# Three changes of order in a hybrid decoder block: ticks of the recurrent heads, weight casts at two gate borders, and weight sums in the first feed-forward product

## The chip, the cores and the metric

The kernel runs on one core of a Trainium2 chip, in one launch. The metric is the device time of one execution in microseconds (us). The time before is 2270.74 us, the median of three runs (2270.26 to 2275.47).

## The reference

One decoder layer on x of 512 tokens by 2048 columns, all in float32. A conditioning vector c gives six rows of shift, scale and gate. A normalised and modulated x goes through one projection whose columns feed two head groups: eight heads of dilated causal attention and eight heads of a gated linear recurrence (HGRN2, state 128). The heads' outputs, the recurrent ones normalised and multiplied by a gate, go through an output projection and a gated residual. Then follows a feed-forward part with the square of ReLU.

```python
def reference(x, c, ...):
    ...
    h = rms_norm(x, norm1_w[l]) * (1.0 + scale1) + shift1
    aq, ak, av, gq, gf, gi, gg = jnp.split(h @ w_in[l], split_at, axis=-1)
    attn = rms_norm(dilated_attention(rope(norm(aq)), rope(norm(ak)), av), attn_out_norm_w[l])
    hg = rms_norm(hgrn2(gq, gf, gi, lb), hg_norm_w[l]) * silu(gg)
    x = x + gate1 * (concatenate([attn, hg]) @ w_out[l])
    h2 = rms_norm(x, norm2_w[l]) * (1.0 + scale2) + shift2
    x = x + gate2 * (square(relu(h2 @ w_ff1[l])) @ w_ff2[l])
```

(The listing is shortened; helper names stand for the reference's own steps.)

## The kernel before, in words

**Products in three parts.** Every large product is made of float32 operands split into a high part (a cast, on ScalarE) and a low part (source minus high part, a subtraction on VectorE). TensorE multiplies high by high, high by low and low by high. `load_w` (line 189) loads two rows of weight tiles at a time, casts them (line 39, `whi`) and makes their low parts (line 40, `wlo`); four pairs of high and low parts exist at a time.

**Projections and ticks.** `project` (line 372) runs over sixteen k; each k is 12 matmuls of 512 columns into four PSUM banks (lines 202 to 204). After each k it calls `tick`, which advances the first generator of the list `tasks` by one step, up to its next `yield`; when a generator ends, the same tick goes on to the next one. A finished projection's banks are copied out by ScalarE (lines 411, 571, 712), and the next projection's first matmuls need those banks. TensorE's instructions run in the order in which the program is written (`manual_schedule`, line 850); so the yields decide between which matmuls a head's blocks stand. The order on the other engines is made at build time by a scheduler that works through a simulated timeline by priorities (`high_priority` raises one); `issue_after(x)` forbids that what is traced inside it, on x's engine, is placed ahead of x.

**A recurrent head** (`hgrn_head`, line 587) builds decay products level by level on VectorE (`z`, lines 603 to 619), and takes twelve ticks: three levels; the blocks of `pA` from the first three levels (line 584); three more; `pB`; one more; `pC` and `pD` with copies on ScalarE; an empty one; `pE` with the copy `far_sb` (line 684); the output product `pho` (line 692). `hgrn` runs four heads. The queue of tasks is the first group of recurrent heads, four attention heads (`attention`, line 449, with three empty ticks in front by `lead`), the second recurrent group, four more attention heads, a norm, `hg_out(0)`, `attention_out` and `hg_out(1)`. `hg_out` and `attention_out` turn finished columns (`to_mix`, line 551, matmuls on `ptm`, then ScalarE's scaled copy `mix`); `split_mix` (line 393) makes high and low parts of a `mix`, the stationary operand of the output projection. The first group's ticks lie beside three projections, 48 ticks; the second group's beside the next but two.

**The two gate borders.** `hg_gate` (line 706) projects the gate columns, once per group. Its four banks are copied by ScalarE (line 712). The first is followed by the second `hg_gate`, the second by `project_out(0)`, the first quarter of the output projection (line 878). There the operand of k = 0 is the first mix.

**The feed-forward products.** After four blocks of the plain kind, both products use a form of seven products for four (Strassen-Winograd). A block has seven parts, in the order 1, 5, 6, 7, 3, 4, 2, each of 48 matmuls (lines 1196 to 1198). Parts 5, 6, 7 and 4 first need a sum of weight tiles (`sum_of`, line 1161, VectorE line 1164), four sums to a part (u = 0 to 3); `part` (line 1166) then makes the high part (ScalarE, line 1180, `vhi`) and the low part (VectorE, line 1181, `vlo`). Each u has one pair of buffers, so a part's high part waits until the matmuls of the part before have read that u. The first product has six such blocks (2 to 7), of which block 2 is called `first` and has its sums behind the eighth low part; the second product follows with blocks of its own. Results are turned and made into forms in between (`turn`, `make_forms`), partly on VectorE, also as steps of `tasks`.

Of the kernel before, what the change touches and what calls it, by code (L numbers as in the profile page):

```python
# [44 lines left out]
def hybrid_block(ctx, tc, x, c, positions, norm1_w, w_ada, b_ada, w_in, q_norm_w, k_norm_w,  # L45
# [140 lines left out]
        nc.sync.dma_start(dst.rearrange("o (r p) -> (o r) p", p=P), row[0:NK, 0:P])  # L186
        yield

    def load_w(view, k0, c0, n=512, eng=None, ahead=True, raws=None, behind=False):
        with tc.high_priority() if ahead else ExitStack():  # L190
            raw = wr.tile([P, 2, n], F32, name="wraw", tag="raw", bufs=4)
            with tc.issue_after(marks[-3].ins) if behind else ExitStack():
                nc.sync.dma_start(raw, view[:, k0:k0 + 2, c0:c0 + n])
            if raws is not None:
                raws[:] = [raw[:, 0], raw[:, 1]]
            return [_split(nc, wr, raw[:, j], n, eng if j else None) for j in range(2)]

    def tok_mm(banks, hi, lo, whi, wlo, first, last):

# [172 lines left out]
    def project(c0, mm, rate=1.85, after=None):  # L372

        banks = [bank("prj", tag="mm") for _ in range(4)]
        for k0 in range(0, NK, 2):
            for j, (whi, wlo) in enumerate(load_w(win_v, k0, c0, 512, None, behind=len(marks) > 2)):
                k = k0 + j
                mm(banks, hhi[k], hlo[k], whi, wlo, k == 0, k == NK - 1)
                tick()
                owed[0] += rate  # L380
                while owed[0] >= 1.0:
                    bg_step()
                    owed[0] -= 1.0
                if after:
                    after(k)
            marks.append(asked[0])
        return banks
# [58 lines left out]
        bgw.insert(0, qk_norm(ts, i, rs))  # L446
        return ts if i else (ts, rs)

    def attention(qr, ks, vs, lead=0):
        qs, rsq = qr  # L450

        place = {3: (0, 0), 2: (1, 0), 0: (1, 384), 1: (2, 0)}

        def heads_t(h):
            tT = []
            for i, src in enumerate((qs, ks)):
                pt = bank("ptq")
                for ti in range(NT):
                    pe.transpose(pt[:, ti * P:(ti + 1) * P], src[ti][:, h * DH:(h + 1) * DH], ident)
                t = work("qT")  # L460
                act.activation(t, pt, AF.Copy, scale=wcol[:, i:i + 1])
                tT.append(t)
            return tT

        def scores(h, qT, kT):
            lsum = sm.tile([P, NT], F32, name="lsum")
            m = sm.tile([P, NT], F32, name="m")
            ps_s = [bank("pscore") for _ in range(3)]
            s_sb = [work("s_sb") for _ in range(3)]
            for ti in (3, 2, 0, 1):  # L470
                n = (ti + 1) * P
                b, o = place[ti]
                pe.matmul(ps_s[b][:, o:o + n], lhsT=qT[:, ti * P:(ti + 1) * P], rhs=kT[:, 0:n], start=True, stop=True)
            for ti in (3, 2, 0, 1):
                n = (ti + 1) * P
                b, o = place[ti]
                s = s_sb[b][:, o:o + n]
                with tc.high_priority(offset=400):
                    dve.scalar_tensor_tensor(s, ps_s[b][:, o:o + n], rsq[:, ti, h:h + 1], lnc_sb[:, 512 - n:512],
                                             op0=ALU.mult, op1=ALU.add)  # L480
                    dve.tensor_reduce(m[:, ti:ti + 1], s, axis=AX.X, op=ALU.max)
                    dve.tensor_scalar(m[:, ti:ti + 1], m[:, ti:ti + 1], -1.0, None, op0=ALU.mult)
                    act.activation(s, s, AF.Exp, bias=m[:, ti:ti + 1], accum_out=lsum[:, ti:ti + 1])
            return s_sb, lsum

        def weights_t(s_sb):
            p_sb = []
            for b, tis in enumerate(((3,), (2, 0), (1,))):
                pT = bank("pT")
                p_sb.append(work("p_sb"))  # L490
                for ti in tis:
                    o = place[ti][1]
                    for sj in range(ti + 1):
                        c = slice(o + sj * P, o + (sj + 1) * P)
                        pe.transpose(pT[:, c], s_sb[b][:, c], ident)
                n = 256 if b == 2 else 512
                act.copy(p_sb[b][:, 0:n], pT[:, 0:n])
            return p_sb

        def values(h, p_sb, lsum):  # L500
            hs = slice(h * DH, (h + 1) * DH)
            po = bank("po")
            for ti in range(NT):
                b, o = place[ti]
                for sj in range(ti + 1):
                    pe.matmul(po[:, ti * P:(ti + 1) * P], lhsT=p_sb[b][:, o + sj * P:o + (sj + 1) * P],
                              rhs=vs[sj][:, hs], start=sj == 0, stop=sj == ti)
            dve.reciprocal(lsum, lsum)
            for ti in range(NT):
                dve.tensor_scalar(qs[ti][:, hs], po[:, ti * P:(ti + 1) * P], lsum[:, ti:ti + 1], None, op0=ALU.mult)  # L510

        for _ in range(lead):
            yield
        tT = heads_t(0)
        yield
        p_sb = None
        for h in range(4):
            if h:
                values(h - 1, p_sb, lsum)
            s_sb, lsum = scores(h, *tT)  # L520
            for _ in range(4):
                yield
            p_sb = weights_t(s_sb)
            yield
            if h < 3:
                tT = heads_t(h + 1)
                yield
        values(3, p_sb, lsum)
        yield
# [54 lines left out]
            pe.matmul(dst[r0:r0 + 32, (b // 4) * 32:(b // 4) * 32 + 32], lhsT=lhs[:, bs], rhs=rhs[:, bs],  # L584
                      start=True, stop=True)

    def hgrn_head(h, f, q, vs, ss):


        hs = slice(h * DH, (h + 1) * DH)  # L590
# [41 lines left out]
        z2 = level(2)  # L632
        yield
        z4 = level(4)
        yield
        pA = bank("pA").rearrange("p (l b t) -> p l b t", l=4, t=32)
        flat = lambda t: t.rearrange("p b t -> p (b t)")
        for i, (l, r) in enumerate(((kk, q), (z1, z1), (z2, z2), (z4, z4))):
# [44 lines left out]
            pe.matmul(pE[:, u * 256:(u + 1) * 256], lhsT=z256[:, u * P:(u + 1) * P], rhs=z256[:, 256:512], start=True, stop=True)  # L683
        act.copy(far_sb[:, 2:6].rearrange("p b t -> p (b t)"), pE)
        yield
        tile_of = {(i, i): AT[:, i] for i in range(4)}
        for i, at in enumerate(((0, 1), (2, 3), (0, 2), (0, 3), (1, 2), (1, 3))):
            tile_of[at] = far_sb[:, i]
# [8 lines left out]
            act.activation(q[:, t], f[:, t], AF.Square, accum_out=ss[:, h, ti:ti + 1])  # L697
        yield

    def hgrn(fs, qs, vs, rs):  # L700
        ss = sm.tile([P, 4, NT], F32, name="hss", bufs=2)
        for h in range(4):
            yield from hgrn_head(h, fs[h], qs[h], vs, ss)
        rstd_of(rs.rearrange("p t h -> p (t h)"), ss.rearrange("p t h -> p (t h)"), 16, 1.0 / DH)

    def hg_gate(ht):
        gb = project(6144 + ht * 512, tok_mm, after=split_early if ht else None)
        gs = []
        for ti in range(NT):
            g = slot("gg")  # L710
            with tc.high_priority():
                act.copy(g, gb[ti])  # L712
            gs.append(g)
        for g in gs:
            sg = wk.tile([P, 512], F32, name="sg", tag="ev", bufs=2)
            act.activation(sg, g, AF.Tanh, scale=0.5)
            dve.tensor_scalar(sg, sg, 0.5, 0.5, op0=ALU.mult, op1=ALU.add)
            dve.tensor_tensor(g, g, sg, op=ALU.mult)
        return gs
# [133 lines left out]
    while bgw:  # L853
        bg_step()
    bgw[:] = later
    tasks.append(hgrn(f0, hq0, hv0, hrs[0]))
    q0 = qk(0, "aq", 0)
    k0_ = qk(1024, "ak", 1)
    v0 = evac(project(2048, tok_mm), "av")
    tasks.append(attention(q0, k0_, v0, 3))  # L860
    hq1 = hgrn_q(1)
    hv1 = evac(project(5120 + 512, tok_mm), "gi")
    tasks.append(hgrn(f1, hq1, hv1, hrs[1]))
# [14 lines left out]
    def project_out(q, rate, after):  # L878
        banks = [bank("prj", tag="bg" if q % 2 and i < 2 else "mm") for i in range(4)]
        for i0 in range(0, NK, 2):  # L880
            for j, (whi, wlo) in enumerate(load_w(wout_v, korder[i0], q * 512)):
                i = i0 + j
                while q == 0 and len(mixp) <= i:
                    if not split_mix():
# [273 lines left out]

    split_done, cast_done, loads = [], [], []

    def sum_of(dst, a, b, first):

        with tc.issue_after(split_done[7].ins) if first else ExitStack():
            dve.tensor_tensor(dst, a, b, op=ALU.subtract)  # L1164

    def part(i, u, w, first):

        b11, b12, b21, b22 = (w[u, e, n] for e in range(2) for n in range(2))
        if i == 5:
            sum_of(b11, b12, b11, first)  # L1170
        if i == 6:
            sum_of(b11, b22, b11, first)
        if i == 7:
            sum_of(b12, b22, b12, first)
        if i == 4:
            sum_of(b11, b11, b21, first)
        src = {1: b11, 5: b11, 6: b11, 4: b11, 7: b12, 2: b21, 3: b22}[i]
        hi = pools[f"spl{u}"].tile([P, 2, 512], F32R, name="vhi")
        lo = pools[f"spl{u}"].tile([P, 2, 512], F32R, name="vlo")
        cast_done.append(act.copy(hi, src))  # L1180
        split_done.append(dve.tensor_tensor(lo, src, hi.bitcast(F32), op=ALU.subtract))  # L1181
        return hi, lo
# [136 lines left out]
    def part_of(item):  # L1319
# [6 lines left out]

        def call(u):
            with tc.high_priority() if first and j < 2 else ExitStack():
                return part(i, u, w, first)
        return call  # L1330

    def order_of(item):
# [107 lines left out]
```

## Time and profile before

| | before |
|---|---|
| median of three runs | 2270.74 us (2270.26 to 2275.47) |
| the profiled execution | 2268.98 us |
| its span | 2267.1 us |
| TensorE's mean granted clock | 0.997 |
| instructions | 33088 |

PE is TensorE, DVE VectorE, ACT ScalarE, POOL GpSimd, SP the engine that issues most loads. A row of the waits says which engine and line waited for whose instruction, then the total in us, the number of waits and the longest. A row of a timeline gives start, duration, engine, line, operation, written and read tiles, and in brackets the idle time ahead and what ended it; equal neighbours are merged (x4). A row of the windows gives the stretch, its length, the busy time of PE, PEld (weight loads), DVE, ACT and POOL, the granted clock of PE, the DMA share and GB/s. Matmuls overlap: one is listed with 0.39 us and the next starts 0.23 us after it.

### The profile page before, as it was taken

The numbers are of one execution on the slowest core, as the hardware profiler recorded it, in microseconds if no ns is written. First come the engines' busy times: TensorE is split into PE (matmuls) and PEld (weight loads), VectorE is DVE, ScalarE is ACT, GpSimd is POOL, SyncE is SP. The second block draws the span as 40 slices with busy tenths as digits, with TensorE's granted clock in tenths as the row PEclk, the third lists the DMA queues.
The fourth block names the chain that finished last, engine by engine and source line by source line (L and its number), as shares of the span: only waits on it lengthen the run. The fifth ranks groups of instructions, "written<-read, shape, count | busy, mean of one in ns | idle before, by whom it ended". The sixth has DMA issues, their size and how long they took to land.

```text
span 2267.1 us, 33088 instructions
## 1 busy us (share of the span) xinstructions
PE 2212.1 (98%) x11769; PEld 1824.7 (80%) x11769; DVE 1808.9 (80%) x2765; ACT 1097.5 (48%) x1950; POOL 439.1 (19%) x664
## 2 busy tenths in 40 slices
PE   4999999999999999999999999999999999999999
PEld 3788787888888888888888888888888888888887
DVE  6998878688876557778658988898897779967878
ACT  5555334443453464457545555564564333443332
POOL 1000022000220000003232323333232222222221
PEclk9999999999999999999999999999999999999999
DMA  9797564566555248737879789889889987998884
GB/s 327 255 333 254 185 197 145 173 199 209 183 167 182 66 152 281 272 115 270 319 283 363 279 309 385 298 290 366 328 292 371 362 315 260 349 346 311 306 294 166
DMA packets 262581, 598.30 MB, mean 264 GB/s; under 512 B 23220, under 2 KB 43968, under 8 KB 262416
## 3 DMA queue, kind: packets, MB, share of 16 engines
q1 hardware_dynamic: 186800, 332.54, 43.2%
q0 software_dynamic: 70720, 254.21, 30.4%
q10 hardware_dynamic: 4896, 9.44, 1.2%
q8 instruction: 93, 1.52, 0.3%
q14 instruction: 72, 0.59, 0.1%
HBM read 518.49 MB, written 77.61 MB: 263 GB/s over the span
## 4 chain that ended last, share of the span: by engine, by line
PE 67%; issue 12%; DMA 9%; DVE 8%; POOL 3%; ACT 1%; SPq 0%; POOLq 0%; DVEq 0%; ACTq 0%
PE f L1198 8%; PE f L1197 8%; PE f L1196 8%; PE prj L202 8%; PE prj L204 8%; PE prj L203 8%; DMA f_lod<-fs 2%; PE f L212 2%; PE f L210 2%; PE f L211 2%; PE prj L211 2%; PE prj L212 2%; PE prj L210 2%; DVE vlo L1181 2%; DMA Fl<-h_lod 2%
## 5 line engine op out<-in xcount | busy, mean ns | idle before, releaser
L1180 ACT CAST vhi<-raw 128x1024 fp32r<-128x1024 f32 x392 | 413.5, 1056 | 534.0 <-PE f L1198 421.9
L1181 DVE TENSOR_TENSOR vlo<-raw,vhi 128x1024 fp32r<-128x1024 f32 x392 | 478.5, 1226 | 150.1 <-ACT vhi L1180 149.3
L1197 PE MATMUL f<-vlo,Fh 128*128 128x512 f32 x1376 | 536.9, 390 | 2.4 <-DVE vlo L1181 2.3
L1198 PE MATMUL f<-vhi,Fl 128*128 128x512 f32 x1376 | 535.7, 389 | 0.9 <-DMA Fl<-f_lod 0.9
L1196 PE MATMUL f<-vhi,Fh 128*128 128x512 f32 x1376 | 536.1, 390 | 0.0
L39 ACT CAST whi<-wraw 128x512 fp32r<-128x512 f32 (+1 forms) x368 | 220.7, 602 | 464.8 <-PE prj L204 330.9
L40 DVE TENSOR_TENSOR wlo<-wraw,whi 128x512 fp32r<-128x512 f32 (+1 forms) x368 | 245.7, 671 | 181.8 <-ACT whi L39 170.5
L202 PE MATMUL prj<-whi,hi 128*128 128x512 f32 x896 | 360.7, 403 | 1.8 <-ACT gg L712 1.7
L204 PE MATMUL prj<-whi,lo 128*128 128x512 f32 x896 | 350.7, 391 | 0.0
L203 PE MATMUL prj<-wlo,hi 128*128 128x512 f32 x896 | 349.8, 390 | 0.0
L1197 PEld LDWEIGHTS f<-vlo,Fh 128*128 128x128 f32 x1376 | 258.3, 188 | 61.0 <-DVE vlo L1181 7.7
L1198 PEld LDWEIGHTS f<-vhi,Fl 128*128 128x128 f32 x1376 | 258.3, 188 | 54.8 <-DMA Fl<-f_lod 1.4
L1196 PEld LDWEIGHTS f<-vhi,Fh 128*128 128x128 f32 x1376 | 258.3, 188 | 53.4
L1164 DVE TENSOR_TENSOR raw<-raw,raw 128x1024 f32<-128x1024 f32 x224 | 269.6, 1225 | 3.3 <-DMA raw<-in_w_ff_dram 2.9
L132 DVE SCALAR_TENSOR_TENSOR acc<-araw,sc,acc 128x512 f32<-128x512 f32 (+1 forms) x392 | 250.4, 677 | 22.9 <-DMA araw<-in_w_ada_dram 22.2
L202 PEld LDWEIGHTS prj<-whi,hi 128*128 128x128 f32 x896 | 168.9, 189 | 36.6 <-ACT gg L712 2.9
L204 PEld LDWEIGHTS prj<-whi,lo 128*128 128x128 f32 x896 | 168.6, 188 | 36.9 <-DVE lo L244 0.3
L203 PEld LDWEIGHTS prj<-wlo,hi 128*128 128x128 f32 x896 | 169.1, 189 | 32.7
L1142 POOL DMA_DIRECT2D Fh<-f_hid x112 | 79.0, 705 | 423.9 <-PE f L1198 410.2
L212 PE MATMUL f<-hi,wlo 128*128 128x512 f32 x256 | 99.9, 390 | 1.0 <-DVE wlo L40 1.0
L210 PE MATMUL f<-hi,whi 128*128 128x512 f32 x256 | 100.3, 392 | 0.0
L211 PE MATMUL f<-lo,whi 128*128 128x512 f32 x256 | 99.6, 389 | 0.0
(311 smaller groups left out, 2910.5 us busy)
## 6 DMA issues: line engine op xcount, KB each, us to landing
raw<-in_w_ff_dram SPq DMA_DIRECT2D x224, 512.0 KB, 10.5
araw<-in_w_ada_dram SPq DMA_DIRECT2D x384, 256.0 KB, 4.6
Fh<-f_hid POOLq DMA_DIRECT2D x112, 512.0 KB, 6.7
Fl<-f_lod POOLq DMA_DIRECT2D x112, 512.0 KB, 7.9
wraw<-in_w_in_dram SPq DMA_DIRECT2D x104, 512.0 KB, 5.0
Fh<-h_hid POOLq DMA_DIRECT2D x60, 512.0 KB, 6.5
Fl<-h_lod POOLq DMA_DIRECT2D x60, 512.0 KB, 7.5
f_hid<-part POOLq DMA_DIRECT2D x48, 512.0 KB, 8.1
```

The costliest lines, as they stand in the source:

```text
L39: nc.scalar.copy(hi, src)
L40: _split.low = (eng or nc.vector).tensor_tensor(lo, src, hi.bitcast(F32), op=ALU.subtract)
L132: dve.scalar_tensor_tensor(acc, raw[:, k - k0], vec[:, k:k + 1], acc, op0=ALU.mult, op1=ALU.add)
L202: pe.matmul(banks[ti], lhsT=hi[:, ts], rhs=whi, start=first, stop=False)
L203: pe.matmul(banks[ti], lhsT=hi[:, ts], rhs=wlo, start=False, stop=False)
L204: pe.matmul(banks[ti], lhsT=lo[:, ts], rhs=whi, start=False, stop=last)
L1164: dve.tensor_tensor(dst, a, b, op=ALU.subtract)
L1180: cast_done.append(act.copy(hi, src))
L1181: split_done.append(dve.tensor_tensor(lo, src, hi.bitcast(F32), op=ALU.subtract))
L1196: pe.matmul(banks[t], lhsT=fh[u][a][:, ts], rhs=whi[:, a], start=first, stop=False)
L1197: pe.matmul(banks[t], lhsT=fh[u][a][:, ts], rhs=wlo[:, a], start=False, stop=False)
L1198: pe.matmul(banks[t], lhsT=fl[u][a][:, ts], rhs=whi[:, a], start=False, stop=end)
```

## The change

Four edits, none of which adds or removes an instruction of the computation.

- `hgrn` takes a `lead` for its first head: the first group's first head has three more empty ticks between its third level and the blocks of `pA`. The first attention group's three empty ticks at its start are taken out.
- The third head (h = 2) of each recurrent group has one more empty tick between `pE` with its copy and the output product.
- `load_w` can place its two casts (and no other instruction) behind the last bank copy of the gate projection made last (`evacuated`). It is used for the second pair of k in every `project` after the first gate, which is the second gate's, and in `project_out(0)`.
- In all blocks of the first feed-forward product but the first one, each weight sum is placed behind the low part made two before it.

```diff
-    def load_w(view, k0, c0, n=512, eng=None, ahead=True, raws=None, behind=False):
+    evacuated = []
+
+    def load_w(view, k0, c0, n=512, eng=None, ahead=True, raws=None, behind=False, cast_behind=False):
...
-            return [_split(nc, wr, raw[:, j], n, eng if j else None) for j in range(2)]
+            with tc.issue_after(evacuated[0].ins) if cast_behind and evacuated else ExitStack():
+                return [_split(nc, wr, raw[:, j], n, eng if j else None) for j in range(2)]
...
-            for j, (whi, wlo) in enumerate(load_w(win_v, k0, c0, 512, None, behind=len(marks) > 2)):
+            for j, (whi, wlo) in enumerate(load_w(win_v, k0, c0, 512, None, behind=len(marks) > 2, cast_behind=k0 == 2)):
...
-    def attention(qr, ks, vs, lead=0):
+    def attention(qr, ks, vs):
...
-        for _ in range(lead):
-            yield
         tT = heads_t(0)
...
-    def hgrn_head(h, f, q, vs, ss):
+    def hgrn_head(h, f, q, vs, ss, lead):
...
         z4 = level(4)
-        yield
+        for _ in range(1 + lead):
+            yield
...
         act.copy(far_sb[:, 2:6].rearrange("p b t -> p (b t)"), pE)
         yield
+        if h == 2:
+            yield
...
-            yield from hgrn_head(h, fs[h], qs[h], vs, ss)
+            yield from hgrn_head(h, fs[h], qs[h], vs, ss, 0 if h else lead)
...
-                act.copy(g, gb[ti])
+                evacuated[:] = [act.copy(g, gb[ti])]
...
-    tasks.append(hgrn(f0, hq0, hv0, hrs[0]))
+    tasks.append(hgrn(f0, hq0, hv0, hrs[0], 3))
...
-    tasks.append(attention(q0, k0_, v0, 3))
+    tasks.append(attention(q0, k0_, v0))
...
-            for j, (whi, wlo) in enumerate(load_w(wout_v, korder[i0], q * 512)):
+            for j, (whi, wlo) in enumerate(load_w(wout_v, korder[i0], q * 512, cast_behind=q == 0 and i0 == 2)):
...
-    def sum_of(dst, a, b, first):
+    def sum_of(dst, a, b, first, tie):
 
-        with tc.issue_after(split_done[7].ins) if first else ExitStack():
+        with tc.issue_after(split_done[7 if first else -2].ins) if first or tie else ExitStack():
             dve.tensor_tensor(dst, a, b, op=ALU.subtract)
...
-                return part(i, u, w, first)
+                return part(i, u, w, first, stage_ == 1)
```

(The four calls of `sum_of` in `part` pass `tie` on.)

More of the change, by code (lines that the diff above doesn't have):

```diff
@@ L698, in hgrn_head, with hgrn @@
         yield
-    def hgrn(fs, qs, vs, rs):
+    def hgrn(fs, qs, vs, rs, lead=0):
         ss = sm.tile([P, 4, NT], F32, name="hss", bufs=2)
         for h in range(4):
-            yield from hgrn_head(h, fs[h], qs[h], vs, ss)
+            yield from hgrn_head(h, fs[h], qs[h], vs, ss, 0 if h else lead)
         rstd_of(rs.rearrange("p t h -> p (t h)"), ss.rearrange("p t h -> p (t h)"), 16, 1.0 / DH)
@@ L1159, in hybrid_block, with part @@
     split_done, cast_done, loads = [], [], []
-    def sum_of(dst, a, b, first):
-        with tc.issue_after(split_done[7].ins) if first else ExitStack():
+    def sum_of(dst, a, b, first, tie):
+        with tc.issue_after(split_done[7 if first else -2].ins) if first or tie else ExitStack():
             dve.tensor_tensor(dst, a, b, op=ALU.subtract)
-    def part(i, u, w, first):
+    def part(i, u, w, first, tie):
         b11, b12, b21, b22 = (w[u, e, n] for e in range(2) for n in range(2))
         if i == 5:
-            sum_of(b11, b12, b11, first)
+            sum_of(b11, b12, b11, first, tie)
         if i == 6:
-            sum_of(b11, b22, b11, first)
+            sum_of(b11, b22, b11, first, tie)
         if i == 7:
-            sum_of(b12, b22, b12, first)
+            sum_of(b12, b22, b12, first, tie)
         if i == 4:
-            sum_of(b11, b11, b21, first)
+            sum_of(b11, b11, b21, first, tie)
         src = {1: b11, 5: b11, 6: b11, 4: b11, 7: b12, 2: b21, 3: b22}[i]
```

## The prediction, on record before the run

> **What bounds the kernel now.** I read first the page, for the busy shares and the slices.
>
> ```profile
> PE 2212.1 (98%) x11769; PEld 1824.7 (80%) x11769; DVE 1808.9 (80%) x2765; ACT 1097.5 (48%) x1950; POOL 439.1 (19%) x664
> PE   4999999999999999999999999999999999999999
> ```
>
> TensorE (PE) is busy 2212.1 us, and outside the first fortieth hardly stops. Its instructions and their order of work stay as they are, so the change can only win what PE stands still or runs slowly after about 100 us. Next the waits of PE, longest in total first; the columns are total, times, longest.
>
> ```profile
> PE pA L584 <- DVE z L611: 4.4, 2, 3.5
> ...
> PE f L1197 <- DVE vlo L1181: 2.3, 6, 0.4
> PE pho L692 <- ACT far_sb L684: 1.9, 2, 1.0
> PE prj L202 <- ACT gg L712: 1.7, 2, 1.3
> ```
>
> Each edit has one of these rows as its object; the longer rows lie in the opening, which no edit touches. Together they hold 10.3 us of idle time. A stall costs more than its idle time, as PE's timeline in the first feed-forward product shows (start, duration).
>
> ```profile
> 1339.62 0.39 PE L1196 MATMUL f<-vhi,Fh 128*128 128x512 f32 x1
> 1339.99 0.50 PE L1197 MATMUL f<-vlo,Fh 128*128 128x512 f32 x1
> ...
> 1342.62 0.39 PE L1196 MATMUL f<-vhi,Fh 128*128 128x512 f32 x1
> 1343.39 0.50 PE L1197 MATMUL f<-vlo,Fh 128*128 128x512 f32 x1 [0.39 <-DVE vlo L1181]
> 1343.73 0.39 PE L1198 MATMUL f<-vhi,Fl 128*128 128x512 f32 x1
> ```
>
> In an undisturbed run such matmuls start 0.23 us apart (255.04 to 255.28 below). Here the steps are 0.77 and 0.34 us: 0.54 and 0.11 too long, 0.65 together for an idle of 0.39. So I add 0.26 us to every wait of a 512-wide stream. The first pair, 0.37 apart, and the following 0.11 lose another 0.25 us that the wait view doesn't list.
>
> **First recurrent head: three ticks before pA.** A tick is one k of a projection, 12 matmuls, 12 x 0.23 = 2.8 us.
>
> ```profile
> 250.02 0.66 PE L584 MATMUL pA<-z 128*32 128x32 f32 x32 [3.48 <-DVE z L611]
> 250.60 0.80 PE L202 MATMUL prj<-whi,hi 128*128 128x512 f32 x1
> ...
> 255.04 0.41 PE L203 MATMUL prj<-wlo,hi 128*128 128x512 f32 x1
> 255.28 0.39 PE L204 MATMUL prj<-whi,lo 128*128 128x512 f32 x1
> ```
>
> After the wait, ten matmuls start in the 4.44 us from 250.60 to 255.04, where ten steps of 0.23 make 2.3: 2.1 us more go to a slow clock. The stall is worth 4.4 + 2.1 = 6.5 us. Will the products be there three ticks later? VectorE (DVE) at that place:
>
> ```profile
> 246.26 0.70 DVE L40 TENSOR_TENSOR wlo<-wraw,whi 128x512 fp32r<-128x512 f32 x1
> 246.87 1.42 DVE L132 SCALAR_TENSOR_TENSOR acc<-araw,s1c,acc 128x512 f32<-128x512 f32 x2
> ...
> 249.54 0.42 DVE L611 TENSOR_TENSOR z<-gq,f 128x256 f32<-128x256 f32 x1
> ```
>
> The last product ends at 249.96. The blocks that read it would without the waits stand at 250.02 - 4.4 = 245.6, and three ticks later at 254.0. With PE running on, though, DVE gets one or two more low parts with two background sums each ahead of that product, 0.70 + 1.42 = 2.1 us apiece: 252.1 to 254.2. It fits, with a margin between 1.9 us and nothing: I take the whole 6.5 us, 2 us of it in doubt. The three ticks issue nothing; the head's later PE blocks, masks and copies just stand three ticks later, behind more projection matmuls. Attention gives its three ticks back, so that it starts only one tick later.
>
> **Third head: one tick before the output product.**
>
> ```profile
> 359.51 2.16 ACT L440 ACTIVATE ak<-ak,rs 128x128 f32<-128x128 f32 x7 [1.93 <-POOL rs L216]
> 361.57 0.56 ACT L684 COPY far_sb<-pE 128x512 f32<-128x512 f32 x1
> ```
>
> ScalarE (ACT) scales keys ahead of the copy that PE needs; the copy is late by 1 us, a tick is 2.8. Both waits go (one per head group): 1.9 + 2 x 0.26 = 2.4 us. In the first group the third head now also stands three ticks further from the key norm; but its middle now meets that norm's ACT and POOL work. I take nothing for that, between a gain and a loss of 1.2 us (one wait as long as this one).
>
> **Casts behind the bank copies at the two gate borders.** ACT around the second border, then PE:
>
> ```profile
> 794.16 0.68 ACT L556 ACTIVATE mix<-ptm,cols 128x512 f32<-128x512 f32 x1
> 794.88 0.62 ACT L243 CAST hi<-mix 128x512 fp32r<-128x512 f32 x1
> 796.85 0.62 ACT L39 CAST whi<-wraw 128x512 fp32r<-128x512 f32 x1 [1.35 <-PE prj L204]
> 797.37 0.68 ACT L556 ACTIVATE mix<-ptm,cols 128x512 f32<-128x512 f32 x1
> 797.95 2.04 ACT L712 COPY gg<-prj 128x512 f32<-128x512 f32 x4
> ```
> ```profile
> 793.44 0.60 PE L554 MATMUL ptm<-ident,gg 128*128 128x128 f32 x4
> ...
> 796.65 0.60 PE L554 MATMUL ptm<-ident,gg 128*128 128x128 f32 x4
> 798.58 0.50 PE L202 MATMUL prj<-whi,hi 128*128 128x512 f32 x1 [1.33 <-ACT gg L712]
> ```
>
> ACT stood idle 1.35 us with a cast at its head that waits for PE, while finished banks waited behind it. With the cast behind the copies this goes: with the smaller wait at the first border (1.7 - 1.3 = 0.4) 1.7 + 2 x 0.26 = 2.2 us. The moved casts, and the low parts on DVE that follow from them, wait for the last copy, 2.04 / 4 = 0.5 us after the gate's last matmul, and are needed two ticks, 5.5 us, after it: the first two weights' matmuls hide them. Uncovered, the two would cost 2 x 0.62 us and a low part, 0.7.
>
> But the extra tick of the third head is never given back in the second group: the whole queue of ticks behind it, attention, gated output, turns of the mix, is one tick late. The first turn (793.44) was one tick ahead of the border; now it is issued at 796.65, directly ahead of the matmuls that read it. From the start of the turn to the end of its cast took 795.50 - 793.44 = 2.06 us; the turning matmuls fill 0.3 of it (798.58 - 1.33 - 0.26 - 796.65); the low part, 0.70 like that of a weight, is read two matmuls or 0.46 after its cast, 0.2 more; 0.26 for starting again: a stall of 2.2 us, and up to 1.2 more if the two casts, marked high-priority, run first. I take 2.6. The second turn has another turn's matmuls behind it, 0.3 us less to wait: 1.9, and either way a little with the order on ACT; I take 1.7. Before, neither existed. Cost: 4.3 us; above, 2.2 + 1.9 + 1.2 = 5.3; below, nothing, if PE is held at the border that long by something else. The value lies near the chain measured.
>
> **Sums behind low parts.** DVE's timeline:
>
> ```profile
> 1335.30 3.50 DVE L1164 TENSOR_TENSOR raw<-raw,raw 128x1024 f32<-128x1024 f32 x3
> 1338.70 1.23 DVE L1181 TENSOR_TENSOR vlo<-raw,vhi 128x1024 fp32r<-128x1024 f32 x1
> 1339.84 2.36 DVE L1164 TENSOR_TENSOR raw<-raw,raw 128x1024 f32<-128x1024 f32 x2
> 1342.11 1.23 DVE L1181 TENSOR_TENSOR vlo<-raw,vhi 128x1024 fp32r<-128x1024 f32 x1
> ```
>
> DVE runs sums of later parts ahead of low parts that PE is about to read. Tied two low parts back, at most two sums can stand ahead. Six waits make 2.3 us, 0.38 each; five are in tied blocks, the sixth in the second product's first block, which isn't tied. 5 x (0.38 + 0.26) = 3.2, and 0.25 in four of the blocks: 4.2 us. The delayed sums hold up a cast on ACT and its low part; the loads on SP wait for the last reader, which is no sum.
>
> **The sum.** 6.5 + 2.4 + 2.2 + 4.2 = 15.3 us won, 4.3 lost: 11.0. The profiled execution took 2268.98 (span 2267.1), 1.8 us under the median; from the median 2270.74 this gives 2259.7.
>
> **Rivals.** A clock that halves again. Two windows (length, then busy PE; PEclk third from the end):
>
> ```profile
> 50.00:52.50 2.50, 0.55 (x5) 0.31 (x3) 2.50 (x8) 2.50 (x7) 0.00 (x0) 1.00 1.09 349
> 53.50:57.00 3.50, 3.50 (x10) 2.68 (x10) 3.50 (x12) 0.95 (x2) 0.00 (x0) 0.52 1.10 351
> ```
>
> Two idle microseconds were followed by 3.5 us at 0.52. The new wait of 2.6 may do this too: ten slow matmuls, 2.1 us, perhaps twice: 2261.8 to 2263.9. Against it: 1.33 us at 798.58 did not. [...]
>
> No new wait: ACT brings the mix in time, or the bank copies were the longer chain anyway. Then 2270.7 - 15.3 = 2255.4.
>
> The waits only move: the edits don't do all they say, since order on DVE and ACT is made anew. Pro: DVE is full around head one, and the margin may be nothing. Head one keeps 2 us and two half-hidden waits of 1.2 appear in the shifted heads: 4.4 less won, 2264.1, with a third 2265.3.
>
> Slower: the sums fall due where DVE has no room.
>
> ```profile
> 1372.30:1383.20 10.90, 10.90 (x50) 9.02 (x49) 9.91 (x13) 4.22 (x4) 3.69 (x6) 1.00 1.04 413
> ```
>
> (DVE is the third busy time, after the length, PE and PEld.) This is product 3 of a block. The four sums for part 4, 4 x 3.50 / 3 = 4.7 us, can no longer run long ahead; here they meet 1.0 us of free time. The 3.7 over must fit between a part's buffer coming free and its use, 36 matmuls = 8.3 us less a cast and a low part of 1.23 each: 5.8. They do, unless over 2.1 us of backlog comes along; from there on PE waits. With all 4.7 on PE in five blocks, 23.5 us: 2283.
>
> **Chances.** Forecast 0.50; no new wait 0.13; slow clock 0.12; waits moved 0.16; sums late 0.09. A measurement of this kernel can tell about 0.3%, 6.8 us. Faster by more: the first two, and nearly all of the slow clock, 0.73; within: the moved waits and the rest, 0.18; slower: 0.09. The range from 2254 (the no-wait case and one wait of 1.2 more) to 2266 (moved waits) leaves out late sums and the mishaps.
>
> **What would show it.** Right: no row for pA on z, far_sb, or gg among PE's waits; full clock at 250 us; low parts in the first product without stalls but for the second product's; a new row of PE on the cast of the mix, two waits of 1.5 to 2.6 us, at the second border. Wrong: no such row, a pA row over 2 us, or stalls at parts 7 and 4.

## The result, and the profile after

| | before | after |
|---|---|---|
| median of 15 runs each | 2270.54 us (2267.97 to 2275.47) | 2266.32 us (2262.57 to 2271.31) |
| ratio of after to before, 95% interval | | 0.998 (0.9973 to 0.9987) |
| the profiled execution | 2268.98 us | 2268.35 us |
| its span | 2267.1 us | 2266.6 us |
| TensorE's mean granted clock | 0.997 | 0.996 |

The change wins 4.2 us (2.9 to 6.1 by the interval), where 11.0 were forecast. The sign was right, the size was not: 2266.32 lies just above the range's upper end of 2266. A win of 4.2 us is less than the 0.3% that the prediction took for the least a measurement can tell; with 15 runs of each kernel the interval of the ratio lies below 1 all the same. (One of the six executions of e1 below took 12616.9 us: e1's median of 2257.09 counts it and would be 2256.97 without it, and its ratio leaves it out.)

The busy shares can't show this; on the page of after, the line of busy times reads

```profile
PE 2211.3 (98%) x11769; PEld 1827.6 (81%) x11769; DVE 1807.2 (80%) x2765; ACT 1098.2 (48%) x1950; POOL 439.5 (19%) x664
```

within 3 us of before on each engine, as it must where only the order changes.

The waits of PE in after, longest in total first (total, times, longest):

```profile
PE prj L205 <- ACT hi L246: 5.8, 2, 4.3
...
PE prj L207 <- DVE lo L247: 2.0, 2, 1.9
PE pt L1230 <- DVE s L1249: 1.8, 1, 1.8
PE f L215 <- DVE wlo L40: 1.6, 2, 1.1
...
PE prj L205 <- ACT aq L414: 0.5, 1, 0.5
...
PE f L1201 <- DVE vlo L1185: 0.4, 1, 0.4
```

All rows that the change aimed at are gone or shrunk as forecast: none for `pA` on `z`, none for `far_sb`, none for `gg`, and one low part (`vlo`) of 0.4 in place of six with 2.3. In their place stand two new ones with 5.8 and 2.0, on the cast and the low part of the mix (line 246 is line 243 of before). They are the late turn of the mix, forecast at 4.3 us for everything; their idle time alone is 7.8.

They lie at the second gate border. PE's timeline of after there (start, duration, and in brackets the idle time ahead):

```profile
786.78 0.60 PE L555 MATMUL ptm<-ident,gg 128*128 128x128 f32 x4
791.66 0.50 PE L205 MATMUL prj<-whi,hi 128*128 128x512 f32 x1 [4.27 <-ACT hi L246]
...
796.53 1.04 PE L555 MATMUL ptm<-ident,gg 128*128 128x128 f32 x8
799.08 0.50 PE L205 MATMUL prj<-whi,hi 128*128 128x512 f32 x1 [1.51 <-ACT hi L246]
...
801.70 0.50 PE L207 MATMUL prj<-whi,lo 128*128 128x512 f32 x1 [1.89 <-DVE lo L247]
```

The turn of the first mix (786.78) is issued directly ahead of the matmuls that read it, as the prediction said; but the wait is 4.27 us and not 2.2 to 2.6. ACT of after in the same stretch tells why:

```profile
787.42 0.69 ACT L557 ACTIVATE mix<-ptm,cols 128x512 f32<-128x512 f32 x1 [5.26 <-PE ptm L555]
788.01 2.04 ACT L716 COPY gg<-prj 128x512 f32<-128x512 f32 x4
789.91 1.18 ACT L39 CAST whi<-wraw 128x512 fp32r<-128x512 f32 x2
790.95 0.66 ACT L246 CAST hi<-mix 128x512 fp32r<-128x512 f32 x1
```

The mix is copied at 787.42, and its high part, which PE waits for, begins only at 790.95: 790.95 - 788.01 = 2.9 us go to four bank copies and the two moved casts, which stand ahead of it. And ACT idled 5.26 us ahead of the scaled copy, with the copies behind it; in e8 below, the first of them runs at 785.05, 3 us earlier. The place at the head of ACT's line that the casts were to give up is now held by the mix.

The last of the three stalls, 1.89 us on a low part, is made on DVE. Both casts that it follows end by 799.55 (798.41 + 1.14), but DVE first runs eight gated products (line 731) and then the low parts (line 247). In e3 below, which leaves the moved casts out, the low parts come first and this stall is missing. DVE of after, then of e3:

```profile
798.87 2.18 DVE L731 SCALAR_TENSOR_TENSOR gg<-f,hrs,gg 128x128 f32<-128x128 f32 x8
800.97 1.28 DVE L247 TENSOR_TENSOR lo<-mix,hi 128x512 fp32r<-128x512 f32 x2
```
```profile
798.03 1.29 DVE L247 TENSOR_TENSOR lo<-mix,hi 128x512 fp32r<-128x512 f32 x2
799.24 2.18 DVE L731 SCALAR_TENSOR_TENSOR gg<-f,hrs,gg 128x128 f32<-128x128 f32 x8
```

Then the clock. Windows of after behind the two longer stalls (stretch, length, busy PE, PEld, DVE, ACT, POOL, then PE's granted clock, DMA share, GB/s):

```profile
792.80:796.20 3.40, 3.40 (x9) 2.63 (x9) 3.40 (x11) 1.23 (x2) 0.00 (x0) 0.51 0.49 154
...
803.00:806.40 3.40, 3.40 (x13) 2.82 (x12) 0.45 (x1) 0.86 (x2) 0.00 (x0) 0.50 0.03 11
```

Twice 3.4 us at half clock. At the full clock 3.4 us hold 15 steps of 0.23 us; here the steps are 0.43 us (PE's matmuls of after start at 792.99, 793.42 and 793.84), so that 8 fit: 7 x 0.23 = 1.6 us lost each time.

The lead and the ties did what they were to do. In the stretch where before had 3.48 us of wait for `pA`, PE of after goes from the projection to the blocks and back without a wait:

```profile
253.30 0.39 PE L207 MATMUL prj<-whi,lo 128*128 128x512 f32 x1
253.62 0.46 PE L585 MATMUL pA<-gq,kk 128*32 128x32 f32 x32
253.89 1.02 PE L585 MATMUL pA<-z 128*32 128x32 f32 x96
254.84 0.51 PE L205 MATMUL prj<-whi,hi 128*128 128x512 f32 x1
```

And DVE in the first feed-forward product has one sum (line 1168) to a low part (line 1185), where before ran three sums and two:

```profile
1335.52 1.22 DVE L1168 TENSOR_TENSOR raw<-raw,raw 128x1024 f32<-128x1024 f32 x1
1336.65 1.22 DVE L1185 TENSOR_TENSOR vlo<-raw,vhi 128x1024 fp32r<-128x1024 f32 x1
1337.79 1.22 DVE L1168 TENSOR_TENSOR raw<-raw,raw 128x1024 f32<-128x1024 f32 x1
```

Two rows of before that bear on the sum, and that the prediction doesn't show:

```profile
PE pD L671 <- DVE z L611: 0.9, 1, 0.9
PE pt L1226 <- DVE s L1245: 0.6, 1, 0.6
```

**The two profiles add up in the main.** Gone: `pA` 4.4, its slow clock 2.1, `pD` 0.9 (a row of before that the prediction had not counted), `far_sb` 1.9, low parts 2.3 - 0.4 = 1.9, restarts of eight stalls at 0.26, and 1.0 hidden beside the low parts: 14.3 us. New: the border 7.8 - 1.7 = 6.1 with one restart more, 0.26, and two slow stretches, 3.2; `aq` 0.5 + 0.26; and beside the change's object, the row on `s` near 1235 us, 1.8 where before had 0.6, with a slow stretch of its own (1237.00 to 1240.00 at 0.52), 1.2 + 1.6; low parts of plain blocks (`wlo`) 1.6 for 1.0. That is 13.7, so 0.6 us should be won; the profiled executions lie 2268.98 - 2268.35 = 0.6 apart.

That this fits to the tenth is luck, since the sum leaves out the opening: the first matmul of the projections behind it starts at 189.99 us in after and at 188.98 in before, 1.0 late already. The starts of one and the same matmul in both traces (found by counting those of its kind) show the terms directly. After is 7.4 us ahead at 611 us of before's time (604.00 for 611.44), 9.4 ahead at 785 (775.90 for 785.27), 0.8 behind at 838 (838.81 for 837.97), 3.6 behind at 1340 (1343.20 for 1339.62) and 0.55 ahead at the last one (2261.04 for 2261.59). So the border costs 10.2, where the rows give 7.8 - 1.3 + 0.26 + 3.2 = 10.0, and the sums with the rest of the products win back 4.1; each term holds within some 0.6 us.

The wait on `s` varied from 0.6 to 2.0 us, though DVE has the same order of instructions ahead of it in all twelve kernels, and the profiled execution of after lies 2.0 us above its median: a typical one has less of this.

### The profile page after: what moved, and what is told of

Same layout as the page of the kernel before. It is cut to its first block, busy times and chain, and to the rows that moved or that the text cites. A ratio compares the mean times of both kernels' runs of the same rounds, so it can differ in the third digit from the quotient of the medians.

```text
span 2266.6 us, 33052 instructions
## 1 busy us (share of the span) xinstructions
PE 2211.3 (98%) x11769; PEld 1827.6 (81%) x11769; DVE 1807.2 (80%) x2765; ACT 1098.2 (48%) x1950; POOL 439.5 (19%) x664
## 4 chain that ended last, share of the span: by engine, by line
PE 73%; issue 10%; DMA 7%; DVE 5%; POOL 3%; ACT 1%; SPq 0%; POOLq 0%; DVEq 0%; ACTq 0%
PE f L1202 9%; PE f L1200 9%; PE f L1201 9%; PE prj L205 9%; PE prj L207 9%; PE prj L206 9%; PE f L215 2%; PE f L213 2%; PE f L214 2%; DMA Fl<-f_lod 2%; PE prj L214 2%; PE prj L215 2%; PE prj L213 2%; DMA Fl<-h_lod 1%; POOL Fl L1146 1%
```

## The experiments

Two theories had a part each from the start. Theory 1: the gain went to the turn of the mix, one tick late, and more dearly than priced. Theory 2: the moved casts stand ahead of the mix on ACT, and that is the loss. A third theory, that a removed wait never gives back what its row says, was tested by the parts alone. Ratios are to the kernel before, run on the same chip beside each; their medians were 2270.70 (e1, e2, e3, e6), 2271.55 (e4, e5, e8, e9) and 2271.76 us (e10, e11).

### The tick given back, and a late tick alone

e1, on the changed kernel: `hg_out(0)` has two empty ticks ahead of its first turn and not three, so that the queue of ticks arrives at the border as before.

```diff
-        for _ in range(3):
+        for _ in range(3 if ht else 2):
```

> The changed kernel, but the first gated output starts after two empty ticks instead of three, so that the first turn of the mix stands one tick ahead of the second gate border again. Theory 1 (the lost tick): PE's waits on the cast and the low part of the mix (5.8 and 2.0 us in the changed kernel's profile) and both stretches of half clock around 792 and 803 us go, about 10 to 11 us; time about 2256, ratio to before 0.993 to 0.995. Theory 2 (the moved casts hold up the mix on ACT): a wait of 2 us or more stays at the border, and the time stays above 2262. Theory 3 (the waits removed elsewhere were never worth their row): the border's waits go, but the time falls by less than 5 us against the changed kernel.

Measured: 2257.09 us, 0.994 (0.9927 to 0.9952). That is 2266.32 - 2257.09 = 9.2 us better than the change with its late turn. Waits of PE of e1 from 770 to 830 us:

```profile
PE prj L205 <- ACT gg L716: 1.3, 1, 1.3
PE prj L207 <- DVE lo L247: 0.7, 1, 0.7
```

Instead of 7.8 us there are 2.0, and no half clock (behind both waits the matmuls start 0.23 to 0.24 us apart, as from 789.15 to 789.38 and from 798.24 to 798.48): 5.8 of idle time, 3.2 of clock and a restart make 9.3 us, against 9.2 measured. But the wait on `gg`, which the moved casts were to end, is back at 1.3. ACT of e1 at the border:

```profile
787.59 0.69 ACT L557 ACTIVATE mix<-ptm,cols 128x512 f32<-128x512 f32 x1 [1.86 <-PE ptm L555]
788.18 2.04 ACT L716 COPY gg<-prj 128x512 f32<-128x512 f32 x4
```

The copies no longer stand behind a cast; they stand behind the scaled copy of the second mix, for whose turn on PE ACT idles 1.86 us.

e2, on the kernel before: one more empty tick in `hg_out(0)` and nothing else.

```diff
-        for _ in range(3):
+        for _ in range(3 if ht else 4):
```

> The kernel before with nothing changed but one more empty tick ahead of the first gated output, so that only the turn of the mix is late. Theory 1: two waits of PE on the mix appear without any of the other edits, together 4 to 8 us, with half clock perhaps 2 to 4 us more; time 2275 to 2281, ratio 1.002 to 1.005. Theory 2: without the moved casts the mix comes in time but for 2 us, which the old wait on the bank copies covers; ratio within 0.999 to 1.001.

Measured: 2277.92 us, 1.0031 (1.0019 to 1.0043): 7.2 us slower than before, by a single empty tick that issues nothing. PE's waits of e2 from 770 to 830 us, and the window behind the longer stall:

```profile
PE prj L202 <- ACT hi L243: 4.8, 2, 3.3
PE prj L204 <- DVE lo L244: 1.0, 1, 1.0
```
```profile
802.90:806.30 3.40, 3.40 (x9) 2.66 (x9) 3.38 (x11) 1.30 (x3) 0.00 (x0) 0.50 0.00 0
```

5.8 us of idle time in place of 1.3 (the first border's 0.4 stays), and one slow stretch: 4.5 + 1.6 + 0.26 = 6.4 of the 7.2, whose interval is 4.3 to 9.8. The starts of the same matmuls agree: 1.9 us later than in before ahead of the border (787.17 for 785.27), 8.5 later behind it (846.43 for 837.97), so 6.6 are lost there. The profiled execution, 2281.37 us, lies 3.4 above the median; it also has a wait of 2.01 us with a slow stretch (at 0.50, last section) in a plain block at 1006 us and one of 1.44 on a low part at 1275. So the late turn costs this much with no other edit present: Theory 1 stands. By the rows the prediction's 4.3 (5.3 at most) was too low, the more so as the 6.4 are net of the old wait on `gg`, which the new one takes in; the interval of the times by itself doesn't exclude it.

### The change without the moved casts

e3, on the changed kernel:

```diff
-..., behind=len(marks) > 2, cast_behind=k0 == 2)):
+..., behind=len(marks) > 2, cast_behind=False)):
...
-load_w(wout_v, korder[i0], q * 512, cast_behind=q == 0 and i0 == 2)
+load_w(wout_v, korder[i0], q * 512)
```

> The changed kernel without the casts placed behind the bank copies; ticks and sums as changed. Theory 1: the waits on the mix stay, 4 us or more in total, and the time is 2264 to 2270. Theory 2: with the casts where they were, the first wait on the mix falls from 4.3 to under 2 us, the half clock there goes, and the time is 2258 to 2262.

Measured: 2261.04 us, 0.9953 (0.9941 to 0.9965): 2266.32 - 2261.04 = 5.3 us better than with the casts. ACT of e3, PE's first stall, and the one slow window:

```profile
788.26 2.04 ACT L716 COPY gg<-prj 128x512 f32<-128x512 f32 x4
790.15 0.66 ACT L246 CAST hi<-mix 128x512 fp32r<-128x512 f32 x1
```
```profile
790.86 0.50 PE L205 MATMUL prj<-whi,hi 128*128 128x512 f32 x1 [3.31 <-ACT hi L246]
```
```profile
792.50:795.90 3.40, 3.40 (x12) 2.62 (x11) 3.40 (x12) 1.64 (x3) 0.00 (x0) 0.50 0.00 0
```

Without the two casts the mix follows the copies at once, and the stall is 3.31 instead of 4.27: shorter by the two casts' 1.0. The second row, on the low part, went altogether (2.0), and with it the second slow stretch (1.6): 3.1 + 1.6 + 0.26 = 5.0 of the 5.3. Theory 2 is right too, as a share: with a late turn the casts edit doesn't win 2.2 us, it loses 5.3. The time came out where Theory 2 had put it, but not by the way that it had told: the first wait fell to 3.31 and not under 2, and the slow stretch behind it stayed. The greater part came from the stall on the low part, which goes with another order on DVE (above); why the order made at build time differs there, no run shows. The rest, 3.31 us of stall, is the turn's own chain with the four copies in it.

### Parts alone

e4, on the kernel before, only the lead: three empty ticks in the first head, three fewer in attention.

```diff
+        for _ in range(1 + lead):
+            yield
...
-    tasks.append(hgrn(f0, hq0, hv0, hrs[0]))
+    tasks.append(hgrn(f0, hq0, hv0, hrs[0], 3))
...
-    tasks.append(attention(q0, k0_, v0, 3))
+    tasks.append(attention(q0, k0_, v0))
```

> The kernel before with only the first edit: three empty ticks moved from the first attention group into the first recurrent head. Theory 1 (PE's lost time at that place is the whole of its worth): the wait of pA on z and the half clock after it go, 6.5 us; ratio 0.9965 to 0.9975, time 2263 to 2265. Theory 3 (the wait moves to a later head): the row for pA goes, other rows of 2 us or more come up in the recurrent heads, and the ratio is over 0.998.

Measured: 2262.35 us, 0.9958 (0.9945 to 0.997): 9.2 us won, 6.8 to 12.5 by the interval, where 6.5 were forecast for the first head. The product is in time, and PE runs the whole stretch at full clock:

```profile
244.00:262.00 18.00, 18.00 (x202) 14.82 (x202) 18.00 (x42) 3.74 (x6) 0.00 (x0) 1.00 0.69 227
```

Its waits from 225 to 830 us:

```profile
PE prj L202 <- ACT gg L713: 1.7, 2, 1.3
PE pho L693 <- ACT far_sb L685: 1.0, 1, 1.0
PE prj L202 <- ACT aq L411: 0.5, 1, 0.5
```

Beside `pA`, the row of `pD` (0.9) is gone and one of the two `far_sb` rows, that of the first group: the three ticks help the heads behind the first one too. 6.5 + 0.9 + 1.0 + 2 x 0.26 - 0.76 for the new `aq` is 8.2.

e5, on the kernel before, only the third head's extra tick:

```diff
         act.copy(far_sb[:, 2:6].rearrange("p b t -> p (b t)"), pE)
         yield
+        if h == 2:
+            yield
```

> The kernel before with only the third heads' extra tick. Theory 1: both waits on far_sb go (2.4 us), and the late turn of the mix comes, worth 7 us when it was made alone; ratio 1.001 to 1.003, so the edit by itself makes the kernel slower, 2273 to 2277. Theory 3 (the late turn belongs to something else): ratio 0.998 to 1.000.

Measured: 2275.11 us, 1.0017 (1.0008 to 1.0027): 3.9 us slower. The `far_sb` rows are gone as forecast, 2.4 us, and the late turn is there (PE's waits of e5 from 225 to 830 us):

```profile
PE prj L202 <- ACT hi L243: 4.8, 2, 3.3
PE pA L584 <- DVE z L611: 4.3, 2, 3.5
...
```

With e2's 7.2 for the turn, 7.2 - 2.4 = 4.8 would be lost; the interval (1.8 to 6.1) holds that. So this edit is a loss by itself, and since e4 takes one of its two waits away with the lead, it wins 1.2 us at most beside it, for the same price.

e6, on the kernel before, only the sums behind low parts in the blocks of the first product:

```diff
-        with tc.issue_after(split_done[7].ins) if first else ExitStack():
+        with tc.issue_after(split_done[7 if first else -2].ins) if first or tie else ExitStack():
             dve.tensor_tensor(dst, a, b, op=ALU.subtract)
```

(`tie` is passed on as in the change.)

> The kernel before with only the sums tied behind low parts. Theory 1 and 2: the five waits on low parts in the tied blocks go, 4.2 us with their restarts; time 2266 to 2267, ratio 0.9975 to 0.9985; the one wait in the second product's first block stays. Theory 3: the waits go from the row, but DVE is late elsewhere (parts 7 and 4, the turns), and the ratio is 0.9990 to 1.001.

Measured: 2267.44 us, 0.9983 (0.9974 to 0.9991): 3.3 us won, where 4.2 were forecast and 2.0 to 5.9 is the interval. From 1240 to 1700 us one low part is still waited for:

```profile
PE f L1197 <- DVE vlo L1181: 0.4, 1, 0.4
```

It is that of the second product, which isn't tied. One more, of 0.3 us, stands ahead of this stretch, at 1230 us in the block called `first`, where before had none. No wait came up at parts 7 and 4. The profiled execution of e6 also has the long wait on `s`, 2.0 us, with a slow stretch at its end (1235.20 to 1238.60 us at 0.51), like that of after.

e10, on the kernel before, only the moved casts (`evacuated`, and `cast_behind` at both borders).

> The kernel before with only the casts placed behind the bank copies. The recorded step says that both waits on gg go: 2.2 us, ratio 0.9985 to 0.9995. The theory that has come out of the runs so far (at the second border the copies stand on ACT behind the scaled copy of a turn, not behind the cast alone) says that the wait of 1.3 us stays and only the 0.4 us at the first border goes: 0.7 us at most, ratio 0.9995 to 1.0005.

Measured: 2274.44 us, 1.0014 (1.0006 to 1.0023): 3 us slower, with the turn in time. Waits of PE of e10 from 225 to 830 us, then ACT at the border:

```profile
...
PE prj L205 <- ACT gg L715: 1.3, 1, 1.3
...
PE prj L207 <- DVE lo L247: 0.7, 1, 0.7
```
```profile
797.62 0.69 ACT L559 ACTIVATE mix<-ptm,cols 128x512 f32<-128x512 f32 x1 [1.87 <-PE ptm L557]
798.20 2.04 ACT L715 COPY gg<-prj 128x512 f32<-128x512 f32 x4
```

(The rows left out are those of `pA`, `far_sb` and `pD`, as before.) The first border's 0.4 is gone and the second's 1.3 stays, behind the mix as in e1; the low part of the mix is new with 0.7. These rows make 0.3 of the 3 us, and the time lies outside both ranges that were expected. The starts of the same matmuls tell where the profiled execution, 4.2 us slower than before's, has the rest: it is 0.3 late at the projections' first matmul and still 0.3 ahead of the second border (785.60 for 785.27), 1.0 behind it (838.97 for 837.97), 3.7 at 1032 us and 4.6 at 1340. So 0.7 are lost at the border that the edit was made for, 2.7 at one wait of 1.86 us on a plain block's low part (`wlo`), more than its idle time, as with a slow stretch behind it (the execution's mean granted clock is 0.996, that of before 0.997), and 0.9 at low parts near 1267 us. DVE has the same order of instructions at that plain block as before, and the `wlo` row varied from 0.8 to 2.3 between the kernels, so this isn't put down to the casts; why the median of twelve executions is 3 us higher stays open.

### The border without a turn in it

e8, on the changed kernel: the first turn stands a tick earlier than before the change, and an empty tick behind the second turn keeps the border's own ticks free of turns. If the copies stand behind the scaled copy of a mix, the wait on `gg` must go now (1a); if something else holds them, it stays (1b).

```diff
-        for _ in range(3):
+        for _ in range(3 if ht else 1):
             yield
...
             to_mix(8 + ht * 4 + h, gs, hs, hgc)
+            if ht == 0 and h == 1:
+                yield
```

> The changed kernel with the first gated output starting two ticks earlier and an empty tick after its second turn, so that no turn of the mix stands in the border's own tick and two mixes are ahead. Theory 1a (the bank copies wait on ACT behind the scaled copy of a turn, which itself waits for PE): the wait of 1.25 us on gg that stayed with the tick given back goes too, 1.5 us with its restart; time 2255 to 2256. Theory 1b (the copies are late for another reason): the wait on gg stays over 1 us, time 2257 as with the tick given back.

Measured: 2254.59 us, 0.9924 (0.9911 to 0.9936), 2.5 us better than e1. All that PE waits for from 225 to 830 us is

```profile
PE prj L205 <- ACT aq L414: 0.5, 1, 0.5
```

and ACT has its first bank copy directly behind the scaled copy, whose turn was a tick ahead:

```profile
784.35 0.69 ACT L557 ACTIVATE mix<-ptm,cols 128x512 f32<-128x512 f32 x1 [1.79 <-PE ptm L555]
785.05 0.59 ACT L716 COPY gg<-prj 128x512 f32<-128x512 f32 x1
```

e9 is e8 without the moved casts (the edit of e3 on top of it).

> As the kernel with the free border, but the casts are not placed behind the bank copies. If the casts are what holds the copies up once no turn is in the way, a wait on gg of 1 us or more comes back at the second border and 0.4 at the first, 2 us: time 2257 to 2258. If the turn alone held them up, nothing changes beyond 1 us, and the cast edit is worth nothing at either border.

Measured: 2253.94 us, 0.9925 (0.9913 to 0.9937), and again only the `aq` row of 0.5. With a border free of turns, the casts need not be moved: PE doesn't wait there with them or without.

e11 is e9 with the sums tied in the second product's first block as well:

```diff
-                return part(i, u, w, first, stage_ == 1)
+                return part(i, u, w, first, stage_ == 1 or blk == (0, 0))
```

> The kernel with the free border and without moved casts, with the sums of the second product's first block tied as well. The last wait on a low part in the feed-forward products goes, 0.9 us; time 2253 to 2254. If the sums there find DVE full, other waits on low parts or forms come up in the second product, and the time is 2254 to 2256.

Measured: 2253.5 us, 0.9928 (0.9915 to 0.994): no difference to e9 that can be told. The wait of 0.4 at the start of the second product went as expected, but not the last one on a low part: one of 0.6 came some 70 us later (1724.28), while e9's wait of 0.8 on a load (`Fl`) is missing. e9 and e11 are the best versions, some 18 us ahead of before and 12 ahead of the change.

## Why the prediction was right in sign and wrong in size

**What the removed waits are worth** was right. The rows that the change was to remove went, and e8, in which no new wait stands at the border, has won 2271.55 - 2254.59 = 17.0 us, 14.5 to 20.2 by its interval; the prediction's 15.3 lies in it, the `gg` waits included. In part this is luck: the lead won more and the sums perhaps less than forecast, and the `gg` waits went with the turn's place and not by the moved casts. So the third theory falls: the rows gave back what they said, restart and clock included.

- *Lead, 6.5:* measured 9.2. The products were in time with a full clock, so the 2 us "in doubt" were not lost. The part alone was sized too low because `pD`'s row was overlooked and because "I take nothing" for the heads behind left out that their `far_sb` wait goes with the lead; in the whole sum that wait is counted, under the third head.
- *Third head, 2.4:* both rows went, but half of that came with the lead already, so that beside it the tick is worth 1.2 us by the rows, for the price of the late turn.
- *Sums, 4.2:* measured 3.3, right within its interval, and 4.1 between the traces of before and after; DVE had room for the delayed sums.

**The step that failed: "a stall of 2.2 us, ... I take 2.6. The second turn ... I take 1.7. Cost: 4.3 us".** The mechanism was foreseen, its place too; the size was off. It measured 7.2 us alone (e2) and 9.2 in the change (after against e1). Three things were missing:

1. The chain was measured on a border where the high part follows the scaled copy at once (2.06 us from turn to end of cast). In the late place, four bank copies of 1.9 us fall due between the two, and ACT runs them first, then the two moved casts, 1.0 us. The prediction had the two casts as "up to 1.2 more" and took 0.4 of it. The copies it had only in a rival, as a chain beside the turn's ("the bank copies were the longer chain anyway"), and not as work ahead of the mix's cast, though it had itself put the copies and the turn into the same tick.
2. The low part. The prediction lets it run right behind its cast. In after DVE runs 2.18 us of gated products ahead of it, and the stall is 1.89 us; in e3 and e1, where it doesn't, the wait on the low part is nothing and 0.7.
3. The clock. The rival "a clock that halves again" came true: 4.27 and 1.89 us of idle time were each followed by 3.4 us at half, 3.2 us in all. The shorter one need not have been followed: 1.97 us near 52 us in the same execution were not (last section). The rival's time of 2261.8 to 2263.9 was still too low, since it kept the short stalls and the 2.2 for the casts.

**The second failing step: "With the cast behind the copies this goes", 2.2 us.** At the second border it didn't. The cast at ACT's head was not the only thing that waits for PE there: with it out of the way the copies stood behind the scaled copy of the mix, whose turn PE issues in the same tick, and the wait stayed 1.3 (e1, e10). The prediction's own lines show it there, at 797.37, between the cast and the copies. Where the turn is out of that tick, the wait is gone with or without the casts (e8, e9). The casts edit was worth nothing in e8, cost 3 us alone (1.4 to 5.2 by the interval, most of it without a shown cause) and 5.3 with a late turn.

So: 9.2 for the lead, 3.3 for the sums, 1.2 for the third head, together 13.7; less 7.2 for the late turn and less 3 to 5.3 for the casts: 1.2 to 3.5, against 4.2 measured (2.9 to 6.1). What stays open is the greater part of e10's 3 us, and the spread of the changed kernel's times, 2262.6 to 2271.3. It would fit slow stretches that come in some executions and not in others: the mean granted clock on record is 0.997 for the three fastest executions and 0.995 for the slowest. But only one execution was profiled.

## What to carry to other kernels

Where one engine's order is written by hand, a tick added anywhere shifts every producer behind it: look for the one that stood just one tick ahead of its reader, and give the tick back before it (here 9 us for one `range`). Price a new wait on the engine that will bring the operand, with everything that is ready there in that tick and may run first, not with the length of the bare chain where it stood before. And before moving an instruction out of the head of a line, look for what stands second: if that waits for the same engine, nothing is won.

## What the runs showed of the hardware

**Behind pauses of about 2 us PE's clock was halved in some places and not in others.** After the first 100 us, the granted clock was 0.50 to 0.52 around the end of these idle stretches of PE or within 2 us behind it: 3.48 us in before, 4.27, 1.89 and 1.82 in after, 3.31 and 2.01 in e2, 3.31 in e3, 2.00 in e6. Each of the three slow stretches in after was 3.4 us long, that in before 6.8 (248.3 to 255.1 us). The clock was 1.00 behind 1.33 us in before (798.00 to 803.00), 1.51 in after (799.00 to 802.50), 1.51 in e2 (809.00 to 812.40) and 1.43 in e3 (798.00 to 801.00). The pause of 2.01 us in e2, and the window behind it:

```profile
1006.52 0.50 PE L212 MATMUL f<-hi,wlo 128*128 128x512 f32 x1 [2.01 <-DVE wlo L40]
```
```profile
1007.70:1011.10 3.40, 3.40 (x10) 2.63 (x9) 1.37 (x3) 2.39 (x7) 0.74 (x2) 0.50 1.00 302
```

In the opening pauses of one length went both ways. Near 52 us PE waits 1.97 us for the same cast (`hi`) in before and in after. Before has 0.52 behind it (the prediction shows the window from 53.50); after runs on at full clock:

```profile
52.90:56.30 3.40, 3.40 (x15) 2.83 (x16) 3.40 (x11) 0.77 (x3) 0.00 (x0) 1.00 1.10 349
```

What tells the two apart was not shown. So in after, stalls near 2 us (1.89 and 1.82) cost 1.6 us of clock more at two places, and at a third (1.97) nothing.
